# An encoder trunk in split float32: right-hand sums and two weight pairs by adding DMAs, another order of the first gated products, idle transposes and a reordered first norm

## The chip, the cores and the metric

One core of a Trainium2 chip. The metric is the device time of one execution in microseconds (us), median of several runs; lower is better. Engines go by the names of the profile: PE (TensorE matmul, PEld its weight load), DVE (VectorE), ACT (ScalarE), POOL (GpSimd), SP (SyncE, which here only issues DMAs).

## The reference

Two layers over a sequence of 512 rows of width 1024. Each layer is a mixer and a feed-forward block, each between RMS norms:

```
h = rms_norm(x, g_pre_mix[l])
z = h @ w_in[l]                       # q | k | v | convB | convC | convX | gate_attn | gate_conv
y_attn = band_attention(q, k, v, sink) @ w_attn_proj[l]
y_conv = (cb * short_conv(cc * cx, conv_w[l])) @ w_conv_proj[l]
mix = (sigmoid(ga) * y_attn + sigmoid(gb) * y_conv) @ w_out[l]
x = x + rms_norm(mix, g_post_mix[l])
h = rms_norm(x, g_pre_ffn[l])
f = (silu(h @ w_gate[l]) * (h @ w_up[l])) @ w_down[l]     # 2816 hidden columns
x = x + rms_norm(f, g_post_ffn[l])
```

Everything is float32.

## The kernel before, in words

**Split operands.** A float32 matrix product is made of three fast ones. Each operand is split into a high half (a cast, on ACT) and a low half (operand minus high half, on DVE); `mm3` (lines 181 to 183) then multiplies high by low, low by high and high by high into one PSUM bank. `split_w` (L130, L131) and `split_to` (L212, L213) are the splits of weights and of activations. `split_by_dma` does without DVE: ACT writes the high half and the negated operand (L135, L136), and a DMA issued by POOL adds the operand to that (L137).

**Seven products for eight.** In the gates of the mixer and in the gated feed-forward product, two weight columns of 128 (a `Pair`: gate and up) meet the activations in a Strassen-like scheme of seven products, numbered 1 to 7. Each has four k-steps of `mm3`, 12 matmuls of 256 columns. The left operands are sums of weight quarters (L438, L417 loads them), the right ones sums of activation quarters (class `Rights`). Products 2, 1, 3 and 5 have right operands in the tile `h`; those of 6, 7 and 4 are sums made later, in `Rights.sums` (L399, L402), and put into tiles named `u`. Product 5 opens a bank and product 3 adds to it once ACT has copied 5 out; 6, 7 and 4 add to the bank of product 1.

**The order of products** is a list made by `orders`: first products 2 and 1 of five pairs (`EARLY`), then product 5 of pairs 0 and 1, then a greedy rule. `run_pairs` walks the list; ahead of each product it splits the weights of the next five (`AHEAD`), and of the next ten those that go by DMA (`by_dma`; before, only product 4 of the mixer gates).

**The boundary.** `down` multiplies the merged mixer output by `w_out`, for four row tiles t of 128, each in two halves of 512 columns. After each tile `after_mix` runs the two norms: ACT sums the squares (L234), DVE adds, POOL takes the power (L228), DVE scales (L270, L242). `Rights.turn` transposes the normed tile on PE (L372) and splits it. Tiles 0 and 1 are turned inside `down`, tile 2 after the first product of the list, tile 3 ahead of the ninth, followed by the sums. The first six weight splits (pairs 0 to 2, `READY` = 3) are made ahead of the norms, in `ahead`.

**The start.** In layer 0 the first row tile of x is loaded by SP and the gain `g` by ACT's queue; ACT sums squares, DVE scales the tile in one instruction (L238), PE transposes it (L250), and the values (V) are multiplied first. This part keeps the order in which it is written on every engine; elsewhere a scheduler orders the instructions of each engine.

Of the kernel before, what the change touches and what calls it, by code (L numbers as in the profile page):

```python
# [28 lines left out]
FT = DFF // P  # L29
EPS = 1e-6  # L30
AHEAD = 5
LEAD = 12
NEG = -1e30
THETA = 500000.0
# [33 lines left out]
def encoder(ctx: ExitStack, tc: tile.TileContext, a, out):  # L68
# [142 lines left out]
    def split_to(h, lo, src):  # L211
        nc.scalar.copy(h, src)  # L212
        nc.vector.tensor_tensor(out=lo, in0=src, in1=h.bitcast(F32), op=ALU.subtract)  # L213
# [134 lines left out]
    class Rights:  # L348
# [39 lines left out]

        def put(self, p, src, cs):
            h, lo = self.op(p)  # L390
            split_to(h[:, :, cs], lo[:, :, cs], src)

        def sums(self, t):

# [10 lines left out]
    class Pair:  # L405
# [3 lines left out]

        def __init__(self, r, w0, c0, w1, c1):  # L410
            self.r, self.at = r, ((w0, c0), (w1, c1))
            self.raw, self.hl, self.done = [None, None], {}, set()

        def load(self, n, raw):
            self.raw[n] = raw
# [11 lines left out]
        def prep(self, p):  # L427

            if p in self.done:
                return  # L430
            self.done.add(p)
            self.need(p)
            l11, l12 = self.raw[0][:, :512], self.raw[0][:, 512:]
            if p not in (2, 1):
                l21, l22 = self.raw[1][:, :512], self.raw[1][:, 512:]
            if p == 5:
                self.sums = [t2([P, 512]) for _ in range(2)]
            add = lambda out, x, y: nc.vector.tensor_tensor(out=out, in0=x, in1=y, op=ALU.add)  # L438
            if p == 2:
                src = l12  # L440
            elif p == 1:
                src = l11
            elif p == 4:
                src = l22
            elif p == 5:
                src = self.sums[0]
                add(src, l21, l22)
            elif p == 6:
                src = self.sums[1]
                add(src, self.sums[0], l11)  # L450
            elif p == 3:
                src = self.sums[0]
                add(src, self.sums[1], l12)
            else:
                src = self.sums[1]
                add(src, l11, l21)
            hl = hl_tile()
            if p in self.by_dma:
                split_by_dma(hl[:, 0], hl[:, 1], src)
            else:  # L460
                split_w(src, hl[:, 0], hl[:, 1])
            self.hl[p] = hl.rearrange("p a (k c) -> p a k c", c=P)

        def product(self, p):
# [16 lines left out]
            if p == 1:  # L481
                nc.scalar.copy(v0, self.a)
                nc.vector.tensor_tensor(out=v2, in0=self.b, in1=v0, op=ALU.add)
            elif p == 5:
                nc.scalar.copy(v1, self.c)
            elif p == 6:
                nc.scalar.copy(v0, self.a)
            elif p == 3:
                nc.vector.tensor_tensor(out=v3, in0=self.c, in1=v0, op=ALU.add)
                self.first()  # L490
            elif p == 7:
                nc.vector.scalar_tensor_tensor(v1, self.a, -1.0, v1, op0=ALU.mult, op1=ALU.subtract)  # L492
            elif p == 4:
                self.second()
# [10 lines left out]
    def orders(n, early):  # L505
# [12 lines left out]
        for i in range(early):  # L518
            seq += [(i, 2), (i, 1)]
            at[i, 2], at[i, 1] = len(seq) - 2, len(seq) - 1  # L520
        for i in range(2):
            at[i, 5] = len(seq)
            seq.append((i, 5))
        opened = early
        while len(seq) < 7 * n:
            left = [i for i in range(opened) if (i, 4) not in at]
# [15 lines left out]
    def run_pairs(pairs, seq, before=lambda n: None):  # L542
        for n, (i, p) in enumerate(seq):
            before(n)
            for j, q in seq[n : n + 2 * AHEAD]:
                pairs[j].need(q)
                if q in pairs[j].by_dma:
                    pairs[j].prep(q)
            for j, q in seq[n : n + AHEAD]:
                pairs[j].prep(q)  # L550
            pairs[i].product(p)
# [9 lines left out]
    for l in range(DEPTH):  # L561
# [44 lines left out]

        if l == 0:
            with in_order(E.PE, E.Activation, E.DVE, E.Pool, E.SP):
                nc.scalar.dma_start(g, a["g_pre_mix"][0].partition_broadcast(P))
                raws = []  # L610
                for t in range(NT):
                    nc.sync.dma_start(normed[t], a["x"][t * P : (t + 1) * P, :])
                    if t < 3:
                        raws.append(load_cols(w_in, *((V0, KV * HD, t * KT // 2) if t < 2 else (K0, P))))
                scale_rows(normed[0], rstd(square_sum(normed[0], D)), g)
                hv = [split_cols(raws[0], KV * HD)]
                r1 = rstd(square_sum(normed[1], D))
                turn(0, normed[0], hT)
                raws.append(load_cols(w_in, K0 + P, P))
                load_constants()  # L620
                scale_rows(normed[1], r1, g)
# [260 lines left out]
        def after_mix(t, accs):  # L882
# [3 lines left out]
            nc.sync.dma_start(dst[t * P : (t + 1) * P, :], x)  # L886
            pre_norm(x, gpr, f)
            normed2[t] = f

        act = [None] * FT  # L890

# [17 lines left out]
        for f in range(FT):  # L909
            pairs.append(Gated(r, a["w_gate"][l], f * P, a["w_up"][l], f * P))  # L910
            pairs[f].f = f

        def ahead():
            for i in range(READY):
# [5 lines left out]
            for i, p in seq[: 2 * READY]:  # L920
                pairs[i].prep(p)

        down(a["w_out"][l], KT, 5, lambda k: (mix[k][:, 0], mix[k][:, 1]), after_mix, lambda t: r.turn(t, normed2[t]), ahead)
        xsrc = dst


# [73 lines left out]
```

## Time and profile before

| | |
|---|---|
| median of 3 runs | 1664.15 us (1663.21 to 1664.96) |
| profiled execution | 1662.62 us, span from first to last instruction 1660.8 us |
| PE busy | 1636.2 us, 99% of the span |
| DVE, ACT, POOL busy | 75%, 56%, 5% |
| mean granted TensorE clock | 0.998 |

The busy share of PE says how long it was not idle; how fast its matmuls followed each other is read from their count in a stretch. An engine's idle time is listed under what it waited for last.

### The profile page before, as it was taken

The page shows a single profiled execution, that of the slowest core. Times are in us where ns is not written, and L with a number is a line of the kernel's source. Part 1 is how long each engine was busy: PE and PEld are TensorE (multiplying, and loading weights), DVE is VectorE, ACT ScalarE, POOL GpSimd, SP SyncE. Part 2 cuts the span into 40 slices and gives each one's busy share as a digit, 9 for nine tenths or more (in the row PEclk, how much of TensorE's full clock was granted, in tenths as well). Part 3 has the DMA queues.
Part 4 walks back from the last instruction along what each step waited for, and adds up shares of the span by engine and source line. Part 5 has one row for each costly group of instructions (what it writes and reads, how often), then busy time and mean ns, then how long its engine had stood idle before and what let it go on. Part 6 is the DMA issues. An engine that isn't in the chain of part 4 may idle for free.

```text
span 1660.8 us, 26449 instructions
## 1 busy us (share of the span) xinstructions
PE 1636.2 (99%) x10033; PEld 1470.2 (89%) x10033; DVE 1237.5 (75%) x2398; ACT 929.5 (56%) x1958; POOL 86.2 (5%) x130
## 2 busy tenths in 40 slices
PE   7999999999999999999999999999999999999998
PEld 7888888889989999988898888888998899999886
DVE  6988876749779988854469788756696898888442
ACT  5666666547656555543346676564575565556331
POOL 0000000000011100000000000000010011001000
PEclk9999999999999999999999999999999999999999
DMA  6322222345652333343413222223457243343332
GB/s 203 95 77 77 64 83 70 89 115 127 183 160 77 102 102 105 116 136 134 148 61 102 76 77 77 77 77 97 101 156 204 92 112 94 104 112 121 108 114 76
DMA packets 249248, 178.63 MB, mean 108 GB/s; under 512 B 5744, under 2 KB 233120, under 8 KB 249120
## 3 DMA queue, kind: packets, MB, share of 16 engines
q1 hardware_dynamic: 246096, 171.18, 35.1%
q0 software_dynamic: 2304, 4.20, 1.6%
q8 instruction: 78, 1.28, 0.3%
q10 hardware_dynamic: 720, 1.57, 0.3%
q14 instruction: 50, 0.41, 0.1%
HBM read 164.34 MB, written 8.39 MB: 104 GB/s over the span
## 4 chain that ended last, share of the span: by engine, by line
PE 96%; DVE 2%; DMA 1%; ACT 1%; issue 0%; POOL 0%; POOLq 0%; DVEq 0%; SPq 0%; ACTq 0%
PE bank L182 30%; PE bank L183 29%; PE bank L181 29%; PE bank L690 2%; PE bank L737 2%; PE bank L724 2%; PE bank L250 0%; DVE u L213 0%; DMA u<-in_w_up_dram 0%; DVE h L213 0%; DMA t<-in_x_dram 0%; ACT t L234 0%; DVE t L438 0%; DVE hl L131 0%; PE bank L372 0%
## 5 line engine op out<-in xcount | busy, mean ns | idle before, releaser
L181 PE MATMUL bank<-h,hl 128*128 128x256 f32 (+1 forms) x1536 | 493.7, 321 | 1.4 <-DVE h L213 1.4
L182 PE MATMUL bank<-h,hl 128*128 128x256 f32 (+1 forms) x1536 | 490.4, 319 | 0.4 <-DVE hl L131 0.4
L183 PE MATMUL bank<-h,hl 128*128 128x256 f32 (+1 forms) x1536 | 490.1, 319 | 0.0
L131 DVE TENSOR_TENSOR hl<-raw,hl 128x512 fp32r<-128x512 f32 x396 | 269.9, 692 | 167.6 <-ACT hl L130 166.2
L130 ACT CAST hl<-raw 128x512 fp32r<-128x512 f32 x396 | 241.8, 620 | 258.8 <-PE bank L183 216.7
L183 PEld LDWEIGHTS bank<-h,hl 128*128 128x128 f32 x1536 | 292.7, 191 | 20.8
L181 PEld LDWEIGHTS bank<-h,hl 128*128 128x128 f32 x1536 | 292.9, 191 | 19.9 <-DVE h L213 2.2
L181 PE MATMUL bank<-u,hl 128*128 128x256 f32 (+1 forms) x976 | 305.6, 313 | 4.1 <-DVE u L213 3.4
L182 PEld LDWEIGHTS bank<-h,hl 128*128 128x128 f32 x1536 | 292.9, 191 | 18.1 <-DVE hl L131 0.6
L182 PE MATMUL bank<-u,hl 128*128 128x256 f32 (+1 forms) x976 | 304.7, 312 | 2.9 <-ACT u L212 1.8
L183 PE MATMUL bank<-u,hl 128*128 128x256 f32 (+1 forms) x976 | 304.1, 312 | 0.0
L181 PEld LDWEIGHTS bank<-u,hl 128*128 128x128 f32 x976 | 186.6, 191 | 15.3 <-DVE u L213 3.8
L182 PEld LDWEIGHTS bank<-u,hl 128*128 128x128 f32 x976 | 186.8, 191 | 13.4 <-ACT u L212 2.2
L183 PEld LDWEIGHTS bank<-u,hl 128*128 128x128 f32 x976 | 186.8, 191 | 10.2
L131 DVE TENSOR_TENSOR hl<-t,hl 128x512 fp32r<-128x512 f32 x240 | 176.9, 745 | 22.5 <-ACT hl L130 19.9
L130 ACT CAST hl<-t 128x512 fp32r<-128x512 f32 x240 | 147.6, 621 | 72.4 <-DVE t L438 47.0
L182 PE MATMUL bank<-hl,u 128*128 128x512 f32 x304 | 118.3, 389 | 0.0
L181 PE MATMUL bank<-hl,u 128*128 128x512 f32 x304 | 118.3, 389 | 0.0
L183 PE MATMUL bank<-hl,u 128*128 128x512 f32 x304 | 118.3, 389 | 0.0
L710 ACT ACTIVATE t<-t,neg 128x256 f32<-128x256 f32 (+1 forms) x128 | 70.4, 552 | 21.1 <-DVE neg L705 20.8
L438 DVE TENSOR_TENSOR t<-t,raw 128x512 f32<-128x512 f32 x112 | 76.7, 696 | 1.2
L906 POOL TENSOR_TENSOR u<-t 128x256 f32<-128x256 f32 x44 | 51.8, 1178 | 398.0 <-DVE t L492 196.9
(137 smaller groups left out, 2275.1 us busy)
## 6 DMA issues: line engine op xcount, KB each, us to landing
raw<-in_w_in_dram SPq DMA_DIRECT2D x88, 512.0 KB, 3.9
u<-in_w_up_dram SPq DMA_DIRECT2D x44, 512.0 KB, 6.1
raw<-in_w_down_dram SPq DMA_DIRECT2D x44, 512.0 KB, 3.5
raw<-in_w_gate_dram SPq DMA_DIRECT2D x40, 512.0 KB, 3.9
raw<-in_w_conv_proj_dram SPq DMA_DIRECT2D x16, 512.0 KB, 4.3
raw<-in_w_attn_proj_dram SPq DMA_DIRECT2D x16, 512.0 KB, 4.3
u<-in_w_in_dram SPq DMA_DIRECT2D x16, 512.0 KB, 5.5
raw<-in_w_out_dram SPq DMA_DIRECT2D x16, 512.0 KB, 3.6
```

Source lines behind the costliest of these rows:

```text
L130: nc.scalar.copy(h, raw)
L131: eng.tensor_tensor(out=lo, in0=raw, in1=h.bitcast(F32), op=ALU.subtract)
L181: nc.tensor.matmul(acc, wh, xl, start=first, stop=False, skip_group_check=goes_on)
L182: nc.tensor.matmul(acc, wl, xh, start=False, stop=False, skip_group_check=goes_on)
L183: nc.tensor.matmul(acc, wh, xh, start=False, stop=last, skip_group_check=goes_on)
L438: add = lambda out, x, y: nc.vector.tensor_tensor(out=out, in0=x, in1=y, op=ALU.add)
L690: nc.tensor.matmul(s[:, :w], q, kk[g][:, 1 - part, lo_b * P : lo_b * P + w], start=part == 0, stop=part == 1)
L710: nc.scalar.activation(p, p, AF.Exp, bias=neg[:, i : i + 1], accum_out=den[:, i : i + 1])
L724: nc.tensor.transpose(pt[:, i * P : (i + 1) * P], p[:, n * P : (n + 1) * P], ident)
L737: nc.tensor.matmul(o, v, hl[:, 1 - part], start=n == 0 and part == 0, stop=kb == hi_b and part == 1)
L906: nc.gpsimd.tensor_tensor(out=out[:, TH:], in0=self.v[:, 1], in1=self.out0[:, TH:], op=ALU.mult)
```

## The change

Six edits. (1) The splits of the right operands 7 and 4 go by DMA. (2) Products 2 and 1 of pairs 3 and 4 are split by DMA too; those of pair 3 are issued right behind the norm of tile 1, those of pair 4 behind `down`, and POOL keeps the written order through `down`. (3) The list of products has 5, 5, 5, 3, 3 (pairs 0, 1, 2, 0, 1) where it had 5, 5; products 3 and 6 may come in either order. (4) Operands that go by DMA are split 8 products ahead where it was 10. (5) At the start PE makes 30 transposes of the identity that nobody reads, and 8 more behind those of tile 0. (6) The gain is loaded on SP's queue behind the first tile; the first tile is scaled in two halves; it is turned, on ACT and DVE too, ahead of the squares of tile 1.

```diff
+FAR = 8
 ...
-            split_to(h[:, :, cs], lo[:, :, cs], src)
+            (split_by_dma if p in (7, 4) else split_to)(h[:, :, cs], lo[:, :, cs], src)
 ...
+            if p == 3:
+                self.prep(6)
 ...
-            elif p == 6:
-                nc.scalar.copy(v0, self.a)
-            elif p == 3:
-                nc.vector.tensor_tensor(out=v3, in0=self.c, in1=v0, op=ALU.add)
-                self.first()
+            elif p in (6, 3):
+                if p == 6:
+                    nc.scalar.copy(v0, self.a)
+                self.halves += 1
+                if self.halves == 2:
+                    nc.vector.tensor_tensor(out=v3, in0=self.c, in1=v0, op=ALU.add)
+                    self.first()
 ...
-        for i in range(2):
-            at[i, 5] = len(seq)
-            seq.append((i, 5))
+        for i, p in ((0, 5), (1, 5)) if early < 3 else ((0, 5), (1, 5), (2, 5), (0, 3), (1, 3)):
+            at[i, p] = len(seq)
+            seq.append((i, p))
 ...
             for j, q in seq[n : n + 2 * AHEAD]:
                 pairs[j].need(q)
+            for j, q in seq[n : n + FAR]:
                 if q in pairs[j].by_dma:
                     pairs[j].prep(q)
 ...
-                nc.scalar.dma_start(g, a["g_pre_mix"][0].partition_broadcast(P))
+                warm(30)          # idle transposes of the identity into a bank of their own
 ...
+                    if t == 0:
+                        nc.sync.dma_start(g, a["g_pre_mix"][0].partition_broadcast(P))
 ...
-                scale_rows(normed[0], rstd(square_sum(normed[0], D)), g)
+                r0 = rstd(square_sum(normed[0], D))
+                for c in (slice(0, 512), slice(512, D)):
+                    scale_rows(normed[0][:, c], r0, g[:, c])
                 hv = [split_cols(raws[0], KV * HD)]
+                turn(0, normed[0], hT)
+                warm(8)
                 r1 = rstd(square_sum(normed[1], D))
-                turn(0, normed[0], hT)
 ...
+            if t == 1:
+                for p in (2, 1):
+                    pairs[READY].prep(p)
 ...
+            if READY <= f < EARLY:
+                pairs[f].by_dma = (2, 1)
 ...
-        down(a["w_out"][l], KT, 5, lambda k: (mix[k][:, 0], mix[k][:, 1]), after_mix, lambda t: r.turn(t, normed2[t]), ahead)
+        with in_order(E.Pool):
+            down(... the same ...)
+            for p in (2, 1):
+                pairs[READY + 1].prep(p)
```

Where instructions go is seen at three places. The lines of the two kernels differ by 1 to 22, so L234 of the one is L235 of the other.

ACT in `down` of layer 0, as tile 0 of the mixer output is done (`bank_4577`, `bank_4578` before and `bank_4619`, `bank_4620` after are its two halves; `u_61_4771` is the gate weight of pair 3). Before:

```order
L234 ACTIVATE t_96_4788,ss_4789<-bank_4577 128x512
L234 ACTIVATE t_97_4795,ss_4796<-bank_4578 128x512
L234 ACTIVATE t_98_4805,ss_4806<-t_93_4783 128x1024
L234 ACTIVATE t_99_4848,ss_4849<-bank_4579 128x512
L234 ACTIVATE t_100_4855,ss_4856<-bank_4580 128x512
```

After the change:

```order
L235 ACTIVATE t_96_4830,ss_4831<-bank_4619 128x512
L136 CAST hl_4915<-u_61_4771 128x512
L137 ACTIVATE hl_4915<-u_61_4771 128x512
L136 CAST hl_4919<-u_61_4771 128x512
L137 ACTIVATE hl_4919<-u_61_4771 128x512
L235 ACTIVATE t_97_4837,ss_4838<-bank_4620 128x512
L235 ACTIVATE t_98_4847,ss_4848<-t_93_4825 128x1024
```

The four instructions of pair 3 have moved in between the squares of the two halves of tile 0.

DVE in the feed-forward of layer 0, up to what pair 0's product 6 reads (its weights are `hl_5222` before and `hl_5294` after; the low half of its right operand is `u_69_5199` before and `u_70_5248` after). Before:

```order
L399 SCALAR_TENSOR_TENSOR u_66_5050<-u_66_5050,u_64_4898 128x4x128
L213 TENSOR_TENSOR u_73_5208<-u_65_4902,u_72_5207 128x4x128
L213 TENSOR_TENSOR u_71_5203<-u_67_5051,u_70_5202 128x4x128
L213 TENSOR_TENSOR u_69_5199<-u_66_5050,u_68_5198 128x4x128
L402 SCALAR_TENSOR_TENSOR u_65_4902<-u_66_5050,u_65_4902 128x4x128
L131 TENSOR_TENSOR hl_5222<-t_109_5058,hl_5222 128x512
```

After:

```order
L441 TENSOR_TENSOR t_111_5209<-t_110_5208,raw_4765 128x512
L400 SCALAR_TENSOR_TENSOR u_66_5109<-u_66_5109,u_64_4948 128x4x128
L132 TENSOR_TENSOR hl_5294<-t_109_5117,hl_5294 128x512
L403 SCALAR_TENSOR_TENSOR u_65_4952<-u_66_5109,u_65_4952 128x4x128
L214 TENSOR_TENSOR u_70_5248<-u_66_5109,u_69_5247 128x4x128
L132 TENSOR_TENSOR hl_5298<-t_108_5116,hl_5298 128x512
```

The subtractions into `u_71` and `u_73` (right operands 7 and 4) are gone from DVE, and weights of later products stand in their place. From the first instruction on tile 2 (L384, after: L385) to the last that product 6 needs, DVE has 33 rows before and 30 after: seven low halves fewer (four of weights, three of right operands), four instructions more (weights of the products 5 and 3 that now come ahead of 6).

PE at the very start, before and after (`t_1_88` is the first tile of x, `bank_96` is read by nobody):

```order
L996 UNCONDITIONAL_BRANCH
L250 MATMUL bank_128<-ident,t_1_88 128x128 x4
L250 MATMUL bank_135<-ident,t_1_88 128x128 x4
L181 MATMUL bank_154<-hl_115,h_86 128x256
L182 MATMUL bank_154<-hl_115,h_86 128x256
```

```order
L1026 UNCONDITIONAL_BRANCH
L620 MATMUL bank_96<-ident 128x128 x30
L251 MATMUL bank_153<-ident,t_1_88 128x128 x4
L251 MATMUL bank_160<-ident,t_1_88 128x128 x4
L620 MATMUL bank_96<-ident 128x128 x8
L182 MATMUL bank_194<-hl_147,h_86 128x256
```

The idle transposes stand ahead of and behind those of tile 0, in the same queue.

## Rows read from the trace of the kernel before

**Rows 1.** The page, part 4: share of the chain that ended last, by engine.

```profile
PE 96%; DVE 2%; DMA 1%; ACT 1%; issue 0%; POOL 0%; POOLq 0%; DVEq 0%; SPq 0%; ACTq 0%
```

**Rows 2.** The waits of PE over the whole execution: line, what it waited for, total us, times, longest us.

```profile
PE bank L250 <- DVE t L238: 9.5, 1, 9.5
PE bank L181 <- DVE u L213: 3.4, 2, 1.7
PE bank L182 <- ACT u L212: 1.8, 2, 0.9
PE bank L182 <- DVE hl L131: 1.5, 4, 0.5
PE bank L181 <- DVE h L213: 1.4, 2, 0.9
```

**Rows 3.** Stretches by time: from and to, length, busy us (and instructions) of PE, PEld, DVE, ACT and POOL, granted TensorE clock, DMA share, GB/s. The first seven are the boundary and the feed-forward of layer 0, the others the same boundary of layer 1.

```profile
480.00:485.00 5.00, 4.13 (x22) 3.19 (x21) 3.71 (x8) 3.45 (x10) 0.71 (x2) 1.00 0.23 94
502.00:504.00 2.00, 1.90 (x16) 1.70 (x15) 2.00 (x4) 1.62 (x4) 0.00 (x0) 1.00 0.00 0
504.00:506.00 2.00, 0.38 (x1) 0.19 (x1) 2.00 (x4) 0.65 (x2) 0.00 (x0) 1.00 0.00 0
506.00:508.00 2.00, 1.12 (x5) 1.15 (x6) 2.00 (x5) 1.24 (x2) 0.00 (x0) 0.63 0.03 8
508.00:510.00 2.00, 2.00 (x12) 2.00 (x11) 2.00 (x5) 0.40 (x2) 0.00 (x0) 0.51 0.01 4
515.00:520.00 5.00, 4.54 (x38) 4.34 (x37) 4.84 (x9) 3.37 (x7) 0.74 (x1) 1.00 1.14 291
530.00:550.00 20.00, 20.00 (x169) 20.00 (x168) 19.82 (x34) 12.57 (x25) 3.91 (x3) 1.00 0.29 75
1300.00:1305.00 5.00, 4.47 (x25) 3.53 (x23) 3.30 (x6) 3.95 (x10) 0.55 (x1) 1.00 0.26 105
1320.00:1325.00 5.00, 4.17 (x35) 3.97 (x34) 5.00 (x9) 4.05 (x9) 0.00 (x0) 1.00 0.01 2
1325.00:1330.00 5.00, 2.86 (x19) 2.48 (x20) 5.00 (x10) 1.83 (x4) 0.00 (x0) 1.00 0.00 0
1330.00:1335.00 5.00, 4.67 (x37) 4.26 (x36) 5.00 (x10) 3.36 (x6) 0.00 (x0) 1.00 0.38 113
1335.00:1340.00 5.00, 4.54 (x38) 4.33 (x38) 4.84 (x9) 3.65 (x7) 0.74 (x1) 1.00 1.16 298
```

**Rows 4.** Instructions in order of time (start us, duration us; in brackets the idle time ahead and its releaser), DVE: three low-half subtractions in one row, in the feed-forward of layer 0.

```profile
503.64 1.89 DVE L213 TENSOR_TENSOR u<-u,u 128x512 fp32r<-128x512 f32 x3
```

**Rows 5.** The same view, ACT and DVE, the norms of the boundary. In order: ACT in layer 0, a pair of casts, then the squares of tile 0's second half; DVE in layer 0, the sum ahead of the power for tiles 1 and 2; then in layer 1 the squares of tile 0's second half and the same two sums.

```profile
490.60 1.14 ACT L130 CAST hl<-u 128x512 fp32r<-128x512 f32 x2
461.58 0.60 ACT L234 ACTIVATE t<-bank 128x512 bf16<-128x512 f32 x1 [0.49 <-PE bank L183]
469.16 0.16 DVE L266 TENSOR_TENSOR v<-ss,v 128x1 f32<-128x1 f32 x1 [0.73 <-ACT t L234]
476.83 0.16 DVE L266 TENSOR_TENSOR v<-ss,v 128x1 f32<-128x1 f32 x1 [0.29 <-ACT t L234]
1282.21 0.58 ACT L234 ACTIVATE t<-bank 128x512 bf16<-128x512 f32 x1
1289.78 0.16 DVE L266 TENSOR_TENSOR v<-ss,v 128x1 f32<-128x1 f32 x1 [0.55 <-ACT t L234]
1297.44 0.16 DVE L266 TENSOR_TENSOR v<-ss,v 128x1 f32<-128x1 f32 x1 [0.29 <-ACT t L234]
```

**Rows 6.** The load of pair 3's gate weight in layer 0: SP's two issues in a row (the first is that of pair 3), and from a view of the DMAs in that stretch, us from issue to landing.

```profile
454.08 3.14 SPq L417 DMA_DIRECT2D u<-in_w_gate_dram  x2
u<-in_w_gate_dram SPq DMA_DIRECT2D x1, 512.0 KB, 6.9
```

**Rows 7.** The instructions that write `hl` on POOL, the adding DMAs of the mixer gates: ns of an issue (least, median, most), and us from issue to landing.

```profile
L137 POOL DMA_DIRECT2D hl<-u x16: 852/860/1032, 360.8 to 1243.5; - x16
DMA to landing us min/median/max: 3.3/4.8/7.3
```

**Rows 8.** The start, instructions in order of time: the identity on POOL, the transposes of tile 0 and the first product on PE, the V weights' casts and tile 1's squares on ACT, tile 1's scaling on DVE; DMA landings of the first tile; and two stretches as in rows 3.

```profile
1.02 0.29 POOL masks.py:199 TENSOR_SCALAR_AFFINE_SELECT ident<-ident 128x128 f32<-128x128 f32 x1
9.46 1.97 PE L250 MATMUL bank<-ident,t 128*128 128x128 f32 x8 [9.46 <-DVE t L238]
11.26 0.58 PE L181 MATMUL bank<-hl,h 128*128 128x256 f32 x1
7.99 1.14 ACT L130 CAST hl<-raw 128x512 fp32r<-128x512 f32 x2 [0.72 <-DMA raw<-in_w_in_dram]
9.29 1.06 ACT L234 ACTIVATE t<-t 128x1024 bf16<-128x1024 f32 x1 [0.16 <-DMA t<-in_x_dram]
12.70 1.27 DVE L238 SCALAR_TENSOR_TENSOR t<-t,r,t 128x1024 f32<-128x1024 f32 x1
14.49 1.29 PE L250 MATMUL bank<-ident,t 128*128 128x128 f32 x8
t<-in_x_dram SPq DMA_DIRECT2D x1, 512.0 KB, 5.3
13.00:14.00 1.00, 1.00 (x6) 1.00 (x6) 1.00 (x2) 1.00 (x3) 0.00 (x0) 1.00 0.99 374
15.00:16.00 1.00, 1.00 (x11) 1.00 (x10) 0.24 (x2) 0.62 (x2) 0.55 (x1) 1.00 1.29 327
```

More of the change, by code (lines that the diff above doesn't have):

```diff
@@ L411, in __init__ @@
             self.r, self.at = r, ((w0, c0), (w1, c1))
-            self.raw, self.hl, self.done = [None, None], {}, set()
+            self.raw, self.hl, self.done, self.halves = [None, None], {}, set(), 0
         def load(self, n, raw):
@@ L608, in encoder, with warm @@
             with in_order(E.PE, E.Activation, E.DVE, E.Pool, E.SP):
-                nc.scalar.dma_start(g, a["g_pre_mix"][0].partition_broadcast(P))
+                idle = bank()
+                def warm(n):
+                    for _ in range(n):
+                        nc.tensor.transpose(idle[:, :P], ident, ident)
+                warm(30)
                 raws = []
@@ L921, in ahead @@
                 pairs[i].prep(p)
-        down(a["w_out"][l], KT, 5, lambda k: (mix[k][:, 0], mix[k][:, 1]), after_mix, lambda t: r.turn(t, normed2[t]), ahead)
+        with in_order(E.Pool):
+            down(
+                a["w_out"][l], KT, 5, lambda k: (mix[k][:, 0], mix[k][:, 1]), after_mix,
+                lambda t: r.turn(t, normed2[t]), ahead,
+            )
+            for p in (2, 1):
+                pairs[READY + 1].prep(p)
         xsrc = dst
```

## Prediction

> **What bounds the kernel now.** I read the chain that ended last first: 96% of it is PE [rows 1], so only time in which PE stands still, or runs at half its clock, can be won. The list of PE's waits comes next [rows 2]: one wait of 9.5 us at the start, and some 8 us on operands that DVE and ACT write (`u`, `h`, `hl`). They lie at two places, which the table of stretches shows [rows 3]: the start of the feed-forward in each layer. In layer 0 PE lacks 0.87 us in 480 to 485 (the first product waits for the second tile's low half), 0.10 + 1.62 + 0.88 = 2.60 in 502 to 508 (pair 0's product 6 waits for its operand and weights) and 0.46 in 515 to 520. DVE has no idle slice there. In layer 1 the same places lack 0.53, then 0.83 + 2.14 + 0.33 = 3.30, then 0.46. Later PE is full: 169 matmuls in 530 to 550, that is 0.118 us each and 1.42 us for a product of 12.
>
> Layer 0 has one more loss. From 506 to 510 the granted clock is 0.63 and 0.51, half of 2.4 GHz, behind PE's longest pause. There 12 matmuls ran in 2 us and 5 in 1.12 busy us, where 0.118 each would take 1.42 and 0.59: 1.1 us lost, and some 0.2 at the edges, so 1.3. Layer 1 paused as long and kept its clock.
>
> **The change, part by part.**
>
> *DVE work ahead of product 6 (edits 1 to 3).* DVE sets the end of both middle waits. Between the first instruction on tile 2 and the last that product 6 needs it has 33 rows before and 30 after: seven low halves go, four instructions of products 5 and 3 come in. Three such subtractions in a row take 1.89 us, with overlap of neighbours 1.8 [rows 4]; so the operand is ready 1.8 us earlier, counted from tile 2. And PE comes to it later, since pair 2's product 5 now stands in front: 1.42 us. Together 3.2 us of cover, against 2.60 us of wait in layer 0 and 3.30 in layer 1: all of the first goes, 3.2 of the second. With the pause in layer 0 the clock's fall should go, 1.3. The waits of 0.46 (weights' low halves, DVE again) should go too: by then all eight subtractions are off DVE, 4.8 us. Sum: 2.60 + 0.46 + 1.3 = 4.4 in layer 0, 3.2 + 0.46 = 3.7 in layer 1.
>
> *What takes the subtractions over.* ACT gets one instruction for each, 1.14 us for two such casts [rows 5]; it is idle for half of 502 to 510 [rows 3], so I cost those behind the norms at nothing. If that cover is gone, PE meets it at product 3, which adds to product 5's bank only after ACT has copied that bank; 0.5 us each then. POOL issues 8 DMAs a layer, 0.86 us each, landing 3.3 to 7.3 us after issue [rows 7]. Operand 7 of tile 3 can be issued some three products ahead of product 6 and is read five products after its start, operand 4 later still: over 8 us against at most 8.2. Pair 4's weights are issued behind the last power, about 490, and read at 498: 8 us too. Nothing then, with a bound of 1 us per layer. POOL's powers of tiles 2 and 3 stand behind pair 3's two DMAs, 1.7 us, but POOL is otherwise idle there. The mixer gates' DMAs go 8 products ahead instead of 10, 11.3 us; again more than 0.86 + 7.3.
>
> *Pair 3's four ACT instructions.* These are not free. They stand between the squares of tile 0's two halves (front matter, ACT), 2 x 1.14 = 2.28 us. In layer 0 ACT idled 0.49 ahead of the second half, so tile 0's sum comes 1.79 us late. The load they read was issued at 454.08 and took 6.9 [rows 6], so it is there at 461.0, when the first half's squares end; a later landing would add to the delay one to one. A late tile 0 is late next for DVE: its chain (sum, power, scale, squares, power, scale) has no slack but DVE's own idle ahead of the sums of tiles 1 and 2, 0.73 and 0.29 [rows 5]. What is left, 1.79 - 1.02 = 0.77, reaches the second tile's low half, for which the first feed-forward product waits. In layer 1 ACT did not idle and DVE's gaps are 0.55 and 0.29: 2.28 - 0.84 = 1.44. So layer 0 keeps 4.4 - 0.77 = 3.6, layer 1 3.7 - 1.44 = 2.2.
>
> *The start (edits 5 and 6).* The first tile landed 5.3 us after its issue and shared the DMA engines with the gain; behind one queue it should come earlier, and PE's transposes of it with it. But the next steps do not move: the V weights are third in the same stream, and ACT casts them at 7.99 (1.14), then tile 0's two high halves (about 1.1), and only then squares tile 1 (1.06, which started at 9.29 before) [rows 8]. That square now ends near 11.4 instead of 10.4; power and scaling behind it (1.27) end at about 13.55, where DVE ended at 13.97, and PE, busy with products, took up the transposes of tile 1 only at about 14.4. So PE continues 0.8 us earlier. It costs nothing that PE itself finishes sooner. The idle transposes lie ahead: at 8 in 1.97 us less gaps, 0.215 each, 30 from 1.35 end at 7.8, before or with the first half of the scaled tile; the 8 behind add 1.7.
>
> What they do to the clock is open. Matmuls of 256 columns ran 6 a us in 13 to 14 and 11 in 15 to 16 [rows 8]: half clock, 1.2 GHz, then full (the clock column shows 1.00 throughout there, but the record starts only at the rise). The rise lies between 14 and 15, some 4.5 us after PE's first work at 9.46. With PE at work from 1.35 I take it as done by 13.6, and the gain as 0.8. Bounds: 1.8 if the V weights land a us earlier; a loss of 1.7 if the transposes do not count, tile 1's interrupt the products, and the slow pace lasts to 18.
>
> The Trainium skill, "TensorE: Matmul & The Clock Gate", Part 4, says that transposes do not count as PE being busy in the way that matmuls do. No row here shows transposes alone, so it can neither be confirmed nor refused; it speaks for the second rival.
>
> **Sum.** 3.6 + 2.2 + 0.8 = 6.6 us from the profiled execution's 1662.6: 1656.0. That execution was 1.5 us faster than the median, so against the median of 1664.15 I say 1657.5.
>
> **Rivals.**
> - *New waits take half.* ACT is late for the copies, or a DMA lands late in each layer; for it speaks that several margins are under 1 us, against it that DVE is still the engine that ends last. Each boundary loses a further 1.5 to 2 us: about 1661.
> - *The idle transposes leave the clock low.* Then the start loses up to 1.7 instead of gaining 0.8: 1657.5 + 2.5 = 1660.0. For it: nothing shows otherwise. Against: before, the rise came some 3 us after the first product at 11.26, and the products come at about 11.3 even so.
> - *Slower.* Pair 3's load lands late. ACT executes in order, so tile 0's norm waits with it, and both feed-forwards start late one to one beyond the slack. DMA was over-full in that stretch already, and w_out's loads move in SP's queue. Gain turns into loss when the landing is later by about 3 us in both layers; at 5 us later it gives 2 x 5 - 6.6 = 3.4 us, 1667.6. Against it: the loads ahead of it are the same ones.
> - *More than forecast.* The delay from pair 3 hides elsewhere, or the runs behind the median, slower than the profile, lost the clock in layer 1 also and now keep it (1.3): 1654.
>
> **Chances.** Forecast 0.45 (1655 to 1660), half 0.15, low clock 0.15, more 0.15, slower than before 0.10. The range takes the sum's upper side (all middle waits and the start's 1.8) at 1653 and, above, leaves out the slower case: 1663. About 0.2% (3.3 us) is what a measurement can tell from no change. Faster by more than that, below 1660.8: forecast, more, low clock and a third of the half case, 0.77, less some for what I do not see: 0.73. Within: 0.19. Slower: 0.08.
>
> **What would show it.** In the profile after: no wait of PE on `u` near 505 and 1326 and the granted clock at 1.00 there; DVE full until the same point; waits of 1.6 and 2.0 us ahead of the first feed-forward product, on `h`; tile 0's second squares at 463.4 less the start's gain. At the start, products at 0.118 us from the first one if the idle transposes lift the clock, tile 1's transposes at about 13.6. It is wrong if PE waits on a tile that a DMA wrote, if ACT ends a wait at product 3, or if the half clock moves to another pause instead of going.

## The result, and the profile after

The changed kernel takes 1652.61 us (median of 6 runs, 1651.67 to 1653.74), the kernel before 1663.26 us in the same session: ratio 0.9934, 95% interval 0.9921 to 0.9947. That is 10.65 us, faster than the 1657.5 forecast and just below the range. In a later session it was 1651.73 against 1662.87, ratio 0.9936 (0.9923 to 0.9949). The first session's profiled execution took 1652.12 us, span 1650.3; PE is busy for 1638.5 us (99%), DVE, ACT and POOL for 74%, 57% and 6%, and the mean granted clock is 1.00.

The waits of PE in the changed kernel (line, releaser, total us, times, longest):

```profile
PE bank L182 <- DVE h L214: 1.9, 2, 1.4
PE bank L620 <- POOL ident masks.py:199: 1.4, 1, 1.4
PE bank L251 <- DVE t L239: 1.2, 1, 1.2
PE bank L182 <- DVE t L497: 0.6, 1, 0.6
PE bank L183 <- DVE h L214: 0.5, 1, 0.5
```

Every wait on `u` or `hl` of [rows 2] is gone. What is left at the boundary is the first feed-forward product's wait on `h` (1.4 us in layer 0, 0.5 in layer 1). The second, third and last line are at the start, and the wait on `t` of L497 is the late up weight of layer 0 in the table below. The stretches that answer to [rows 3] (from and to, us, busy us and instructions of PE, granted clock, DMA share, GB/s):

```profile
480.00:485.00 5.00, 3.63 (x20) 1.00 0.25 97
500.00:505.00 5.00, 5.00 (x43) 1.00 1.19 130
505.00:510.00 5.00, 5.00 (x44) 1.00 0.85 119
515.00:520.00 5.00, 5.00 (x44) 1.00 0.91 243
1295.00:1300.00 5.00, 4.63 (x25) 1.00 0.34 129
1300.00:1305.00 5.00, 4.82 (x41) 1.00 0.37 105
1320.00:1325.00 5.00, 5.00 (x44) 1.00 0.89 97
1325.00:1330.00 5.00, 5.00 (x42) 1.00 0.87 223
```

PE is full where it stood still before, and the granted clock no longer falls.

To see where the time went I paired matmuls: the n-th from the end of one execution with the n-th from the end of the other, and took the difference of their starts. It grows where the change gains and falls where it loses. The steps, in us ("middle" is the stretch of pair 0's product 6 and the wait behind it, on the time of the kernel before 498 to 525 and 1318 to 1345):

| place | forecast | after | after, 2nd execution (e13) |
|---|---|---|---|
| start | +0.8 | +1.20 | +1.13 |
| first feed-forward product, layer 0 | -0.77 | -0.49 | -0.21 |
| boundary's middle, layer 0 | +4.4 | +4.88 | +4.90 |
| some 170 us on, a late up weight | 0 | -0.82 | 0.01 |
| first feed-forward product, layer 1 | -1.44 | -0.02 | -0.31 |
| boundary's middle, layer 1 | +3.7 | +4.88 | +4.88 |
| some 160 us on, a late up weight in before | 0 | +0.87 | +0.87 |
| sum | 6.6 | 10.5 | 11.3 |

The places were right; the sizes were not, and the two late weights were not in the sum at all.

### The profile page after: what moved, and what is told of

The parts are those of the page before. It is cut to its first block, busy times and chain, and to the rows that moved or that the text cites. A ratio compares the mean times of both kernels' runs of the same rounds, so it can differ in the third digit from the quotient of the medians.

```text
span 1650.3 us, 26580 instructions
## 1 busy us (share of the span) xinstructions
PE 1638.5 (99%) x10071; PEld 1473.4 (89%) x10071; DVE 1226.6 (74%) x2383; ACT 936.1 (57%) x1974; POOL 98.8 (6%) x146
## 3 DMA queue, kind: packets, MB, share of 16 engines
q8 instruction: 79, 1.29, 0.3%
q10 hardware_dynamic: 576, 1.05, 0.2%
## 4 chain that ended last, share of the span: by engine, by line
PE 66%; DVE 2%; DMA 1%; issue 1%; ACT 0%; POOL 0%; SPq 0%; POOLq 0%; DVEq 0%; ACTq 0%
PE bank L182 21%; PE bank L183 21%; PE bank L184 21%; PE bank L708 1%; PE bank L755 1%; DMA u<-in_w_up_dram 1%; PE bank L742 1%; DVE hl L132 1%; DVE t L441 0%; PE bank L373 0%; PE bank L251 0%; DVE t L271 0%; ACT t L235 0%; DVE h L214 0%; DVE t L243 0%
## 5 line engine op out<-in xcount | busy, mean ns | idle before, releaser
L132 DVE TENSOR_TENSOR hl<-t,hl 128x512 fp32r<-128x512 f32 x240 | 180.7, 759 | 22.4 <-ACT hl L131 20.9
L713 DVE CUSTOM_DVE_ANT_0 t<-bank,tab,sink 128x256 f32<-128x256 f32 (+1 forms) x128 | 65.7, 542 | 6.1 <-PE bank L708 5.9
```

The lines of the kernel that those rows point to most:

```text
L132: eng.tensor_tensor(out=lo, in0=raw, in1=h.bitcast(F32), op=ALU.subtract)
L713: nc.vector.tensor_tensor_reduce(out=p, in0=s[:, :w], in1=mask[:, m0 : m0 + w], scale=HD**-0.5, scalar=sink[:, h : h + 1], op0=ALU.add, op ...
```

## Experiments

Where an experiment is the changed kernel with something taken back, a diff shows what; the steps quoted are those of the pairing above, against the kernel before.

### The start: four kernels

**e1_start_only** is the kernel before with edits 5 and 6, **e2_boundary_only** the changed kernel without them.

> The kernel before with only the start changed (idle transposes, first norm in two column pieces, gain vector loaded by SP, the square sum of tile 1 later). Theory A, the clock: the identity transposes alone lift TensorE's granted clock at about 6 us, the first products run at 118 ns from 11 us on, tile 1's V products begin at about 14.3 us for 15.54 before: 1.2 us less, 1662.1 us. Rival B, the idle transposes do nothing for the clock and the gain at the start came from the norm in pieces alone: the record rises at about 14 us as before, and the time is 1662.7 to 1663.3 us. The two stalls at the boundary's middle in both layers stay as before in either theory.

> The changed kernel with the start of the kernel before. Theory A, the parts are separate and add up: the boundaries hold 10.65 - 1.2 = 9.4 us, so 1653.8 us; no TensorE wait between the second and the sixth first product in either layer, clock 1.00 there. Rival C, part of the 9.4 us is chance in when the w_up loads of the middle of the FFN land (0.85 lost in layer 0 and 0.87 won in layer 1 in the two profiles, which cancel): the time still 1653.8 within 0.9, with such a wait elsewhere. Rival D, the start is worth more than 1.2 us: above 1654.5 us.

**e3_no_idle_transposes** is the changed kernel with

```diff
-                idle = bank()
-                warm(30)
...
-                warm(8)
```

and **e4_idle_transposes_only** the kernel before with just these lines added.

> The changed kernel without the 38 identity transposes and their bank, all else kept. Theory A: the granted clock rises only some 4 us after the first real transposes, at about 14 us; the V products of tile 0 run at 236 ns until then, tile 1's products begin about 15.3 us, and the time is 1653.6 to 1653.8 us, 1.0 to 1.2 us above the changed kernel. Rival B (the norm in pieces did it): the time of the changed kernel, 1652.6 us, and tile 1's products at 14.4 us, since they wait for VectorE in either case.

> The kernel before with only the 30 + 8 identity transposes added, the first norm and its loads as before. Theory A: the granted clock rises at about 6 us with nothing but transposes executed; the first products run at 118 ns. How much of that lasts depends on when tile 1's columns are ready: if the clock holds them up all of 1.2 us is won (1662.1 us), if VectorE does, less (1662.6 us). Rival B: the clock rises at 14 us as before and the time is 1663.3 us.

Measured on one chip, with 1662.6 for the kernel before: 1662.45 with the start alone (0.9997, 0.9988 to 1.0006), 1652.62 with the boundary alone (0.9940, 0.9927 to 0.9952), 1652.32 without the idle transposes (0.9940, the same interval), 1662.77 with them alone (0.9999, 0.9990 to 1.0007). So the boundary holds the whole gain that can be measured, 10 us. Theory A, a start worth 1.2 us, failed by the time in e2 and e3, for which it said 1653.8 and 1653.6 or more; e1 and e4 lie between their theories.

Yet the transposes do lift the clock. PE in e4 (columns as above; the granted-clock column reads 1.00 before the record's first entry, so there the count of instructions tells the pace):

```profile
4.00:5.00 1.00, 1.00 (x6) 1.00 0.96 336
5.00:6.00 1.00, 1.00 (x9) 1.00 0.91 260
6.00:7.00 1.00, 0.93 (x9) 1.00 1.11 394
9.00:10.00 1.00, 0.56 (x3) 0.53 1.13 370
10.00:11.00 1.00, 1.00 (x7) 0.50 1.02 400
12.00:13.00 1.00, 1.00 (x9) 0.77 1.25 315
```

With nothing run but transposes of the identity the pace rises from 6 to 9 a us; PE then stands idle for 2.5 us, and the record shows 1.2 GHz from 9 to past 12. By the Trainium skill, "TensorE: Matmul & The Clock Gate", Part 4, transposes do not count as PE being busy in the way matmuls do; e4 disagrees, for these float32 transposes at least (whether they run in the mode that the page describes, the trace does not show), and the measurement decides.

The lift is not safe either. In the new start PE has two longer pauses, of 0.54 and some 1.2 us, between 10.2 and 13.5. In 3 of the 13 profiled executions with the new start (those of e8, e11 and e16) the clock fell again there; PE in e16:

```profile
12.00:13.00 1.00, 0.28 (x3) 1.00 1.24 314
13.00:14.00 1.00, 0.54 (x3) 0.79 1.05 383
14.00:15.00 1.00, 1.00 (x7) 0.50 1.06 326
16.00:17.00 1.00, 1.00 (x7) 0.50 1.07 384
```

The start's step is +1.05 to +1.20 in ten of the thirteen and -0.33 to -0.55 in these three, 0.78 on average. The old start varies too: 0.19 in e2 and 0.78 in e15 against the 0 of before, 0.3 on average of the three; without idle transposes (e3) it is 0.74, with them alone (e4) 0.62. The new start is worth some 0.5 us on average, too little for these runs to tell from nothing.

### The boundary: its three edits in all combinations

The edits are S (sums of products 7 and 4 by DMA), Q (pairs 3 and 4 by DMA) and O (the new order). All six kernels have the new start.

**e5_no_sum_dmas** (Q and O):

```diff
-            (split_by_dma if p in (7, 4) else split_to)(h[:, :, cs], lo[:, :, cs], src)
+            split_to(h[:, :, cs], lo[:, :, cs], src)
```

**e6_no_pair_dmas** (S and O):

```diff
-            if t == 1:
-                for p in (2, 1):
-                    pairs[READY].prep(p)
...
-            if READY <= f < EARLY:
-                pairs[f].by_dma = (2, 1)
...
-            for p in (2, 1):
-                pairs[READY + 1].prep(p)
```

**e8_old_order** (S and Q):

```diff
-        for i, p in ((0, 5), (1, 5)) if early < 3 else ((0, 5), (1, 5), (2, 5), (0, 3), (1, 3)):
+        for i, p in ((0, 5), (1, 5)):
```

**e9_order_only**, **e10_sum_dmas_only** and **e11_pair_dmas_only** take two of these back and keep one.

> The changed kernel with the right-hand sums of products 7 and 4 made by ScalarE and VectorE again (behind the norms), not by adding DMAs; pairs 3 and 4 by DMA and the new order kept. Theory A, what the DMAs take off ScalarE and VectorE between the norms counts: the operands of later first products come late again and 1 to 3 us of the gain of about 9.7 us at the two boundaries are lost: 1653.6 to 1655.6 us. Rival E, the order alone removes the stall, since products 7 and 4 come last for every pair: 1652.6 us.

> The changed kernel with pairs 3 and 4 prepared by VectorE as in the kernel before (their left-hand sums of products 2 and 1 not by adding DMAs, nothing prepared ahead for them). Theory A: VectorE has four more sums (1.9 us for the three of the row of the kernel before, 0.6 each) to make within the boundary, and TensorE waits for pair 3's or 4's at about 15 us into it: 1 to 3 us more, 1653.6 to 1655.6 us; the first product of layer 0 comes 0.5 us earlier, since pair 3's ScalarE instructions no longer stand inside the norm. Rival E: VectorE has slack there once the right-hand sums are gone, and the time is 1652.1 to 1652.6 us.

> The changed kernel with the old list of the first products (pairs 0 and 1's product 5 only, the rest by the planner's rule), the DMAs kept. Theory A, the wait at the boundary's middle came from product 5 or 7 of a pair whose sums stand behind the norms; with these sums made by DMAs, but asked for earlier, about half of it comes back: 1655 to 1658 us. Rival E, the order does all of it: the wait comes back whole in both layers, 1661 to 1662 us. Rival G, the DMAs do all of it: 1652.6 us.

> The changed kernel with neither of its adding DMAs: of the boundary's edits only the new order of the first products is left (and the start). Without the sums' DMAs 1656.24 us, without the pairs' DMAs 1656.25 us, with neither by theory A (each edit removes waits of its own, so losses add up: 3.6 + 3.6 on 1652.6): 1659.9 us. Theory H, the edits need each other (the DMAs only free time that the other one's instructions take up again): the order alone wins nothing, 1662.4 us. Theory J, they overlap (each fills the same hole): below 1658 us.

> The changed kernel with the old order and without the pairs' DMAs: of the boundary's edits only the right-hand sums by DMA (and the start). Theory A: 1652.6 + 3.6 (pairs) + 3.8 (order) = 1660.0 us, with the wait in the boundary's middle mostly kept. Theory H: 1662.4 us. Theory J: below 1658 us.

> The changed kernel with the old order and the right-hand sums by ScalarE and VectorE: of the boundary's edits only pairs 3 and 4 by DMA (and the start). Theory A: 1652.6 + 3.6 (sums) + 3.8 (order) = 1660.0 us. Theory H: 1662.4 us. Theory J: below 1658 us. If the four ScalarE instructions of pair 3 cost what the prediction said (0.77 and 1.44 us at the first products) and the order is needed to gain from the DMAs, it is slower than the kernel before: 1664 us.

Measured (medians; ratio to the kernel before; steps in the two middles):

| edits | us | ratio (95%) | layer 0, layer 1 |
|---|---|---|---|
| none (e1) | 1662.45 | 0.9997 (0.9988 to 1.0006) | -1.15, 0.01 |
| O (e9) | 1663.93 | 1.0003 (0.9994 to 1.0012) | -1.65, -1.62 |
| S (e10) | 1667.40 | 1.0029 (1.0018 to 1.0041) | -2.53, -3.33 |
| Q (e11) | 1657.87 | 0.9969 (0.9956 to 0.9981) | 2.27, 2.26 |
| S, O (e6) | 1656.25 | 0.9961 (0.9947 to 0.9974) | 2.76, 2.76 |
| Q, O (e5) | 1656.24 | 0.9964 (0.9951 to 0.9976) | 2.70, 2.69 |
| S, Q (e8) | 1656.45 | 0.9964 (0.9951 to 0.9976) | 4.31, 4.31 |
| all | 1652.61 | 0.9934 (0.9921 to 0.9947) | 4.88, 4.88 |

As the last of three, each is worth 3.6 to 3.8 us by the medians, which are of different sessions, and 4.5 to 5 us by the ratios; their intervals are 2 us wide to either side. For e5 and e6 that is more than the 1 to 3 us of their theory A, for e8 it lies within it. In the two middles together S as the last is worth 4.4, Q 4.2, but O only 1.1. The rest of what e8's profile lacks lies elsewhere, in the low clock of its start and in waits on up weights further on; that the old order brings these is not shown. Alone only Q gains; S costs 5 us, and O gains nothing. So theory A (losses add up) failed for S and O; H (they need each other) holds for O, S alone is worse than any theory said, and Q alone, at 1657.87, is better than A's 1660.0 and just within J's bound. One thing stays untested: all rows but the first also have edit 4, POOL's written order and the weights of product 6 made ahead of those of product 3, which no run takes back.

Why S loses alone is in e10's waits, and in the chain that ended last in layer 0:

```profile
PE bank L182 <- DMA u<-u: 7.4, 2, 3.7
PE bank L182 <- DVE u L214: 3.4, 2, 1.7
```

```profile
502.64 1.55 POOL u L138
504.19 7.04 DMA u<-u
511.23 0.14 issue
511.36 0.55 PE bank L182
```

PE stands for 3.7 us, in each layer, at a product whose right operand a DMA still writes. The old wait of 1.7 on `u` is there too. With DVE's subtractions gone the transfer ends last: it takes 7.04 us, and it is issued late. POOL's issues in e10, and the first in the changed kernel:

```profile
501.60 3.94 POOL L138 DMA_DIRECT2D u<-u  x3 [12.88 <-DVE h L214]
```

```profile
497.89 1.31 POOL L138 DMA_DIRECT2D u<-u  x1 [6.46 <-ACT u L137]
```

In the changed kernel these DMAs are issued at 497.89 to 505.25 and nobody waits for one. In e10 DVE, which has the weights of pairs 3 and 4 to split as well, starts the first sum (L400) at 498.23 instead of 494.94, and the transfer on the chain goes out third, at 504.19 instead of 501.60. The old order by itself is not the cause: e8 has it too, and there, beside the pairs' DMAs, PE waits for no DMA.

O alone meets DVE at the next place, the weights' low halves for the thirteenth product of the list (by its place pair 2's product 5, which now stands ahead of 6) and for the one behind it; DVE makes the first of them at 504.96, behind five subtractions for right-hand sums that start at 500.14 (e9's list, and PE in order of time):

```profile
PE bank L183 <- DVE hl L132: 6.7, 4, 2.8
```

```profile
505.69 0.39 PE L183 MATMUL bank<-h,hl 128*128 128x256 f32 x1 [2.76 <-DVE hl L132]
508.10 0.58 PE L183 MATMUL bank<-u,hl 128*128 128x256 f32 x1 [0.57 <-DVE hl L132]
```

The clock has its part in these losses. In e9, behind the pause of 2.76, the stretches read (columns as above):

```profile
505.00:510.00 5.00, 3.73 (x21) 0.71 0.01 2
510.00:515.00 5.00, 5.00 (x29) 0.61 0.34 99
```

The record shows 1.2 GHz for 6.8 us in each middle of e9, for 3.4 and 6.8 us in e10, for 6.8 and 3.4 in e1, and for none in e5, e6, e8, e11 and the changed kernel. The runs of e9 go with it: 1659.74 us at a mean granted clock of 0.999, 1661.94 to 1662.30 at 0.997, 1663.65 to 1664.63 at 0.996 and 0.995. That O gains nothing alone thus hangs on the clock, as far as one run can tell: the one that kept it is 2.9 us faster than the median of the kernel before.

### What a wait costs

The kernels with all three edits gained 4.88 to 4.90 in each middle (after, e2, e3, e13, e14, e15), whatever their start; only e16, with ACT in written order, gained 4.70 and 4.44. The idle time there, which I had summed, is 2.60 + 0.46 in layer 0 and 3.30 + 0.46 in layer 1 [rows 3]. PE of the kernel before in layer 1, the matmul ahead of each wait and the one behind it (start, duration; idle ahead in brackets):

```profile
1323.89 0.28 PE L183 MATMUL bank<-h,hl 128*128 128x256 f32 x1
1325.86 0.39 PE L181 MATMUL bank<-u,hl 128*128 128x256 f32 x1 [1.68 <-DVE u L213]
1327.15 0.36 PE L182 MATMUL bank<-u,hl 128*128 128x256 f32 x1 [0.91 <-ACT u L212]
...
1328.54 0.28 PE L181 MATMUL bank<-h,hl 128*128 128x256 f32 x1
1329.20 0.39 PE L182 MATMUL bank<-h,hl 128*128 128x256 f32 x1 [0.38 <-DVE hl L131]
...
1330.61 0.28 PE L181 MATMUL bank<-u,hl 128*128 128x256 f32 x1
1331.06 0.39 PE L181 MATMUL bank<-u,hl 128*128 128x256 f32 x1 [0.17 <-ACT hl L130]
1331.61 0.39 PE L182 MATMUL bank<-u,hl 128*128 128x256 f32 x1 [0.17 <-DVE hl L131]
```

From start to start these gaps are 1.97, 1.29, 0.66, 0.45 and 0.55, where the pace is 0.12: 4.32 lost, while the brackets add up to 3.31. A row is 0.28 long and the next starts after 0.12, so the idle time in brackets begins 0.16 after PE could have gone on; with a longer first row behind a wait, each costs 0.16 to 0.26 more than its bracket. With the sixth (0.46 in brackets, 0.62 lost) it is 4.94 for layer 1, near the 4.88 won.

Layer 0 gained the same 4.88, though the sums differ: there the clock fell at the second wait (506.53 to 509.94), rows followed each other after 0.21, and the three short waits of layer 1, 1.30 from start to start, did not come. The low clock and the short waits cost the same, one or the other. e1, whose boundary is that of the kernel before, had the fall in layer 1 as well, and its step there is 0.01. Where the clock stayed low for 6.8 us, it cost 1.15 and 1.17 more (e1 in layer 0, e4 in layer 1).

### The load behind pair 3's and 4's casts

**e7_pair4_dma_only** takes pair 3 off the DMAs:

```diff
-            if t == 1:
-                for p in (2, 1):
-                    pairs[READY].prep(p)
...
-            if READY <= f < EARLY:
+            if READY < f < EARLY:
```

**e12_pair4_early_load** does so too, and loads pair 4's gate weight ahead of pair 3's:

```diff
-            for i in range(READY, EARLY):
+            for i in (READY + 1, READY):
                 pairs[i].load(0, unit([P, 1024], F32))
```

> The changed kernel with pair 4 alone by adding DMAs, pair 3 as in the kernel before: its four ScalarE instructions no longer stand inside the norm. Theory A: 0.5 us of the wait before the first product of layer 0 come back, and if VectorE can make pair 3's two sums in its slack the time is 1652.1 us; if it can't, TensorE waits 0.6 to 1.3 us for them and the time is 1652.7 to 1653.4 us. Rival F, the norms' delay was never due to pair 3: first product where it is in the changed kernel, 1652.6 us.

> The run with pair 4 alone by DMA again (1661.38 us), with one difference: pair 4's gate weight is loaded ahead of pair 3's, in the place where pair 3's stands. There, pair 4's four ScalarE instructions stood in the first tile's norm and waited until 461.88 us for its load, 1.83 us of ScalarE's idle time, and the first product waited 3.2 us. Theory K, the place of the load did it: the load lands about 1.6 us earlier, the first product of layer 0 waits about 1.4 us as in the changed kernel, the clock does not fall there, and the time is 1655 to 1657 us, near that without both pairs' DMAs (1656.25). Rival L, the missing DMA of pair 3 did it: 1661 us again.

e7 missed its expectation by far: 1661.38 us (1657.76 to 1663.56, 0.9990, 0.9981 to 0.9999), 9 us worse than the changed kernel, in runs that go with the granted clock (1657.76 and 1658.03 at 1.000, 1663.56 at 0.995). It puts pair 4's four casts where pair 3's stood, and their weight lands later. ACT and PE in e7:

```profile
461.88 0.62 ACT L136 CAST hl<-u 128x512 fp32r<-128x512 f32 x1 [1.83 <-DMA u<-in_w_gate_dram]
463.98 0.57 ACT L235 ACTIVATE t<-bank 128x512 bf16<-128x512 f32 x1
485.80 0.58 PE L182 MATMUL bank<-h,hl 128*128 128x256 f32 x1 [3.19 <-DVE h L214]
```

and in e12, where the load alone is moved:

```profile
460.10 0.62 ACT L136 CAST hl<-u 128x512 fp32r<-128x512 f32 x1
462.20 0.57 ACT L235 ACTIVATE t<-bank 128x512 bf16<-128x512 f32 x1
484.04 0.39 PE L182 MATMUL bank<-h,hl 128*128 128x256 f32 x1 [1.39 <-DVE h L214]
```

1.78 us later at the casts is 1.78 later at the squares of tile 0's second half and 1.76 at the first product: one to one, as the slower rival said. In e7 PE's pause of 3.19 us also put the clock at 0.50 in 486 to 488; the step there is -3.85 in layer 0 and -2.37 in layer 1. By the two runs that kept the clock, some 3.5 of the 9 us are the clock's. With the earlier load the time is 1655.22 (0.9957, 0.9945 to 0.9970), as theory K expected.

### The changed kernel again, and three attempts at the first product's wait

**e13_after_again** is the changed kernel. **e14_early_loads** moves a load:

```diff
-            pairs[0].load(1, unit([P, 1024], F32))
             for i in range(READY, EARLY):
                 pairs[i].load(0, unit([P, 1024], F32))
+            pairs[0].load(1, unit([P, 1024], F32))
```

**e15_early_loads_old_start** is the same without edits 5 and 6. **e16_act_in_order** keeps ACT in written order through the output projection:

```diff
-        with in_order(E.Pool):
+        with in_order(E.Pool, E.Activation):
```

> The changed kernel itself again, for comparison with the three others on the same chip: 1652.6 us. Where its profile differs from the first one shows what differs from execution to execution: theory C says the first product of layer 1 comes 0 to 1.3 us late and a wait for a weight half in the middle of the feed-forward (0.6 to 0.9 us) comes or not.

> The changed kernel with the gate weights of pairs 3 and 4 loaded ahead of pair 0's up weight. Theory M, the delay of the first products is that of pair 3's late load: the four ScalarE instructions no longer wait, what is left is their own 2.1 us less ScalarE's idle time there; layer 1's first product comes at the same distance from its norm as without pair 3's DMAs, and 0.3 to 0.9 us are won on average: 1651.7 to 1652.3 us. Rival N, the instructions themselves are the delay: 1652.6 us. Against it: pair 0's up weight now lands later, and its splits stand ahead of the second products; if these wait, 1653 us or more.

> The run before this one (weights of pairs 3 and 4 loaded earlier) with the start of the kernel before. Theory A, the start is worth the 1.2 us that the traces show at tile 1's products: 1.2 us slower than that run. Rival P, the feed-forward's own waits give it back (operands there hang on loads and on VectorE, not on when TensorE began): no difference that can be measured, under 0.5 us.

> The changed kernel with ScalarE too in written order through the output projection: pair 3's four instructions stand behind tile 1's squares, where ScalarE idled 3.5 us, no longer inside tile 0's norm. Theory Q, their place is the delay: the first product of layer 0 waits 0.9 us as in the kernel before, not 1.4, layer 1's comes 0 to 1.3 us earlier: 1651.3 to 1652.1 us. Rival N2, tile 2's copies and casts, which the written order moves too, take the delay's place: 1652.6 us or more.

Measured: 1651.73, 1651.79 (0.9938, 0.9926 to 0.9950), 1652.57 (0.9946, 0.9932 to 0.9960) and 1653.98 (0.9947, 0.9933 to 0.9960). In e14's profile the first products come as theory M said, with steps of +0.27 and -0.01 for -0.21 and -0.31 in e13, but its median is that of e13: neither theory is settled by the time, and no version that beats the changed kernel was found. e15 against e14, 0.8 us, is less than either's own spread (1651.15 to 1659.64; 1650.61 to 1655.34). e16 fits rival N2: moved behind tile 1's squares, the casts stand ahead of tile 2's squares, which start at 477.12 where e13 has 474.97 (1.5 us of that is e16's slow start), and the steps are -0.37 and -0.71. e15's theories, 1.2 us or under 0.5, stay open.

The delay in layer 1 follows one load, the gate weight of pair 2, whose cast stands ahead of tile 0's squares on ACT. In the changed kernel and in e2, the casts of that weight and the squares of tile 0's second half:

```profile
1274.58 1.14 ACT L131 CAST hl<-raw 128x512 fp32r<-128x512 f32 x2 [2.47 <-DMA raw<-in_w_gate_dram]
1278.43 0.57 ACT L235 ACTIVATE t<-bank 128x512 bf16<-128x512 f32 x1
```

```profile
1275.78 1.14 ACT L131 CAST hl<-raw 128x512 fp32r<-128x512 f32 x2 [2.41 <-DMA raw<-in_w_gate_dram]
1279.60 0.57 ACT L235 ACTIVATE t<-bank 128x512 bf16<-128x512 f32 x1
```

Put on PE's time of the kernel before (the cast's start plus the steps gained by then), with the delay of layer 1's first product:

| kernel | cast at | delay |
|---|---|---|
| e5 | 1279.03 | 0.00 |
| after | 1279.34 | 0.02 |
| e13 | 1279.89 | 0.31 |
| e3 | 1280.15 | 0.61 |
| e2 | 1280.74 | 1.14 |

The other kernels with pair 3's casts in this place fall in line (e8 1279.03 and 0.00, e11 1278.94 and 0.01, e15 1280.22 and 0.53). Layer 0 goes with the same load: cast at 458.55 (e3), 459.26 (e2), 459.49 (e13) and 459.81 (after), the steps are +0.32, 0.00, -0.21 and -0.49. No run moved this load alone. That it sets the delay is read from how cast and delay go together over these executions; an experiment has not shown it.

## Why the prediction was too small

The forecast counted from the median of three runs, 1664.15; over six runs the kernel before has 1663.26. That is 0.9 of the 4.9 us between 1657.5 and 1652.61. The other 4.0 are gain, 10.65 for 6.6, and the pairing of the profiles shows where two terms failed: the price of the middle waits, 1.7 us, and the cost of pair 3's four ACT instructions, 1.7 us.

**The boundary's middle.** The mechanism held: product 6 no longer waits, no clock falls, and the waits of 0.46 went. The step that failed is the price of the waits, 2.60 + 0.46 and 3.2 + 0.46, taken from idle time: from start to start layer 1 lost 4.94. With the clock's 1.3, layer 0 was worth 4.9 for 4.4, layer 1 4.9 for 3.7: 1.7 us of the miss. The clock's term was of the right size, but it was no extra of layer 0, since the short waits of layer 1 cost as much. That DVE's cover would just suffice in layer 1 (3.2 against 3.30) was too careful; all of the wait went. What was not seen is that the three edits carry each other: priced as DVE rows taken away, S would have been a gain alone, and it is a loss of 5 us.

**Pair 3's four ACT instructions.** Right in kind, but not one figure (in layer 0 0.49 us for 0.77 in the first profile, 0.21 in e13, nothing in e2, a gain of 0.32 in e3; without pair 3 and 4 by DMA, e6, the steps are -0.01 and 0.02). In layer 1 the term of 1.44 measured 0.02 and 0.31, in other kernels up to 1.14. The step that failed took one execution's landing of pair 2's weight (ACT never idle in [rows 5]) for the kernel's own; it was a late one, cast at 1280.58 where the table above has 1279.03 to 1280.74, and ACT has slack whenever the weight comes earlier. That is 1.4 us of the difference to the profile of after, and 0.3 more in layer 0.

**Loads further on.** Nothing was set down for them. Single waits on an up weight come and go: -0.82 in layer 0 of after and not in e13; +0.87 in layer 1, where it was the profile of before that had the wait, and e1, without a boundary edit, gains the same 0.87. They are chance of an execution, not of the change. In the forecast they would have been a width, not a term.

**The start.** 0.8 forecast; 1.2 in the profiles of after, about 0.5 on average over the old start, nothing that a time can show. That transposes lift the clock was right (e4). That the clock then stays was not always so, and e3 shows that 0.74 comes without them.

**The rivals.** New waits did not come in the whole change, but they are what e9 and e10 show: the weights' low halves, and a DMA that lands late. The slower rival's mechanism is real and one to one (e7, e12); in the changed kernel pair 3's load was in time. "More than forecast" (1654) was the nearest. Its two reasons are partly on record: pair 3's delay was hidden in ACT's slack in layer 1, and slower runs of the kernel before do have the lower clock (beside e1 six at a mean of 0.996 took 1663.25 in the median, ten at 0.998 1662.09). But 10.5 us of the gain are in the profiles, so the larger part is the price of the waits, which it had not named. The chances for "faster" add up to 0.80, not 0.77.

## What to carry to other kernels

Price a stall from the starts of the matmuls around it and their pace, since idle time leaves out 0.16 to 0.26 us of each wait here. Where several edits feed one engine, price them together: the sums' DMAs lost 5 us alone and won 3.6 us or more as the last of three, where the pairs' DMAs let DVE make their operands 3.3 us earlier. Before a landing seen once goes into a sum, ask what the path would be with it a us earlier and later.

## What was not expected of the hardware

POOL's issue of an adding DMA takes 1.28 us (median of eight) for a sum of activations, for 0.86 with weights [rows 7]; landing after the issue took 4.3 us in the changed kernel, and 6.3 with three issued in a row (e10; medians of four), 7.04 for the one on the chain. By the fit in the Trainium skill, "DMA: Bandwidth & Descriptors", section "Anatomy of one DMA — SWDGE (gpsimd) path", 2.0 us and 436 GB/s, 256 KB would take an estimated 2.6 us; these rows are above it. After pauses of similar length the clock fell in one execution and stayed in another: layer 0 and layer 1 of the kernel before, and the start of e16 and of after.
